# Hybrid encoder block: v's second half between the keys, the substitution beside z, query decays made in the scans

## Chip, cores and metric

The kernel runs on one core of one Trainium2 chip. The metric is the device time of one execution in microseconds; the value given is the median of three timed runs. A profile of one more execution goes with it.

## What is computed

One layer of an encoder block over 1024 tokens of width 1024, all in float32: a half step of SwiGLU, a mixer, another half step of SwiGLU, and a final row norm. The change is in the mixer and in the row norms.

```python
x = x + 0.5 * swiglu(rmsnorm(x, ffn1_norm), ...)
h = rmsnorm(x, mix_norm); p = h @ w_in
u_a, v_a, qkv, z, b_raw, a_raw = split(p)
# group A: layernorm of gelu(v), 8 groups x 64, a 128x128 causal matrix per group over 128 tokens
y_a = gelu(u_a) * (W_s @ layernorm(gelu(v_a), ln_g, ln_b) + b_s)
# group B: 4 heads x 128, chunks of 64 tokens
q, k, v = silu(causal_dwconv(qkv, conv_w)); q, k = l2norm(q), l2norm(k)
decay = exp(g_i - g_j) for i >= j
L = strict_lower(beta * (k @ k.T) * decay)        # solved: (I + L) sol = rhs, per chunk
u_c, w_c = sol(beta * v), sol(beta * k * exp(g))
attn = lower((q @ k.T) * decay)
# scan over chunks: v_new = u - w S;  o = (q exp(g)) S + attn v_new;  S = S exp(g_last) + k_dec.T v_new
x = x + concat(y_a, rmsnorm(o) * silu(z)) @ w_out
x = x + 0.5 * swiglu(rmsnorm(x, ffn2_norm), ...);  return rmsnorm(x, final_norm)
```

## The kernel before

Every large matmul is made from three float32r products (high times high, high times low, low times high), so weights and activations are split into a high and a low part: a cast on ScalarE (ACT) and a subtraction on VectorE (DVE). `split` does that (L61, L62). TensorE (PE) does the products (L53), GpSimd (POOL) small elementwise work, SyncE (SP) issues most transfers. The two feed-forward blocks (`ffn`) run before and after the mixer; the mixer is `middle`, from about 690 to 1077 us of the span. A tile framework draws all semaphores and orders each engine's instructions at compile time, by the order in which the program states them and by its own estimate of when each is ready. Each engine works through its queue in that order.

In `middle`, `hT` holds the transposed activations. `token_steps` makes 256 columns of a projection for eight tiles of 128 tokens, 24 matmuls of 128x256 each; `proj_steps` makes one 128-wide block of q, k or v for all 1024 tokens, in two halves of 24 matmuls of 128x512, each followed by a causal convolution: a copy into `pad` on ACT (L869), four passes on DVE (L871, L873), a Silu on ACT (L875). Weights come through `load_w` (a transfer, then a split, four buffers `wk`).

The order of the work is this:

1. v's first 256 columns (`v0`), spilled to DRAM; meanwhile beta and the log decays, and `decay(h)` for the four heads. Per head and half it makes two 512-wide tables from a row `grb` that a transfer spreads over the partitions: `EL` for the keys and `EA` for the queries, each by a subtraction, an addition and one Exp (L797 to L803). The two halves share the additions between DVE and POOL.
2. `keys(h)` for four heads: the key projection, two tiles of z's second half as filler (`fill`), then for both halves the transposes (L844), a squared norm on ACT (L896), 1/norm (L880 on DVE, the power L70 on POOL), scalings (L898 to L903), the Gram product, the matrix L (L908), and stores to DRAM. The tiles of the keys are called `kst`.
3. The rest of z; `substitute`, 31 pairs of dependent DVE instructions (L920, L922) on 32x32 blocks that come back from DRAM in another layout, and go out again through DRAM (`xz_d`).
4. v's second 256 columns (`tm("v", 1, ...)`), each tile with Gelu and the layer norm `mix` (L1077 to L1084); per pair of tiles `spatial`, 16 matmuls and a bias (L1094).
5. The value and query projections of head 0, then the scans: eight halves, each with `inverse` (which needs the substitution's result, `Z`), `values`, `queries` and `scan`, woven by hand with the projections of the next heads and with u.

The banks of PSUM in the mixer: two for `ax` (transposes, `spatial`, small products), three for `mm` (projections), one each for `sc`, `sq` and `sd`. The pool `xp` has eight buffers of 128x1024, of which `EL` and `EA` took all; `kst` has three, `aT`, `rv` and `u` two each.

The row norm is `rstd_of`: Square with accumulation on ACT (L74), scale and epsilon on DVE (L76), power on POOL (L70). `fin` is the final norm; its last tile is done in two halves (L655 to L661).

Of the kernel before, what the change touches and what calls it, by code (L numbers as in the profile page):

```python
# [17 lines left out]
P = 128  # L18
# [12 lines left out]
def block_kernel(ctx: ExitStack, tc, a, out):  # L31
# [39 lines left out]

    def rstd_of(src, junk, n):
        ms = sm.tile([P, 1], F32, tag="ms", name="ms", bufs=4)
        nc.scalar.activation(junk, src, AF.Square, accum_out=ms)  # L74
        rs = sm.tile([P, 1], F32, tag="rs", name="rs", bufs=4)
        nc.vector.tensor_scalar(rs, ms, 1.0 / n, EPS, op0=ALU.mult, op1=ALU.add)  # L76
        rpow(rs, rs, 1)
        return rs
# [479 lines left out]
    with ExitStack() as f2:  # L558
# [85 lines left out]
        def fin(t, xt):  # L644
            o = gp.tile([P, D], F32, tag="gsp", name="o", bufs=7)
            if t < 7:
                normed(xt, st["gf"], o)
                nc.sync.dma_start(odram[t], o)
                return

            halves = slice(0, 512), slice(512, D)
            ms = sm.tile([P, 2], F32, tag="ms2", name="ms2")
            rs = sm.tile([P, 1], F32, tag="rs", name="rs", bufs=4)
            for i, f in enumerate(halves):
                nc.scalar.activation(o[:, f], xt[:, f], AF.Square, accum_out=ms[:, i:i + 1])  # L655
            nc.gpsimd.tensor_tensor(rs, ms[:, 0:1], ms[:, 1:2], op=ALU.add)
            nc.gpsimd.tensor_scalar(rs, rs, 1.0 / D, EPS, op0=ALU.mult, op1=ALU.add)
            rpow(rs, rs, 1)
# [19 lines left out]
def middle(tc, nc, a, L):  # L678
# [4 lines left out]
    bank, mm, mm3, split, rpow = L["bank"], L["mm"], L["mm3"], L["split"], L["rpow"]  # L683

    csa = kp.tile([P, NCONST - 1, P], F32, tag="kst", name="csa", bufs=3)
    nc.scalar.dma_start(csa, a["cst"][:, P:].rearrange("p (c n) -> p c n", n=P))
# [97 lines left out]
    EL, EA = {}, {}  # L784

    def decay(h):
        EL[h], EA[h] = (xp.tile([P, 2, 512], F32, tag="x", name="E") for _ in range(2))
        for hf in range(2):
            cs = slice(h * 8 + hf * 4, h * 8 + hf * 4 + 4)
            grb = lv.tile([P, 512], F32, tag="VT", name="grb", bufs=4)  # L790
            nc.sync.dma_start(grb, grd[:, cs.start * P:cs.stop * P].to_broadcast([P, 512]))
            lv_, av_ = v4(EL[h][:, hf]), v4(EA[h][:, hf])

            def mask(i):
                return K(i).unsqueeze(1).to_broadcast([P, 4, P])

            nc.vector.tensor_tensor(av_, v4(grb), b4(gc[:, cs]), op=ALU.subtract)  # L797
            eng = nc.vector if hf else nc.gpsimd
            eng.tensor_tensor(lv_, mask(C_ML), v4(grb), op=ALU.subtract)
            eng.tensor_tensor(lv_, lv_, b4(gc[:, cs]), op=ALU.add)  # L800
            nc.scalar.activation(lv_, lv_, AF.Exp)
            nc.vector.tensor_tensor(av_, av_, mask(C_MA), op=ALU.add)
            nc.scalar.activation(av_, av_, AF.Exp)  # L803
# [81 lines left out]
    def keys(h, fill):  # L885
        kst = [kp.tile([P, 3, 512], F32, tag="kst", name="kst", bufs=3) for _ in range(2)]
        proj_conv(4 + h, [k[:, 0] for k in kst])
        for _ in range(2):
            next(fill, None)
        for hf in range(2):  # L890
            KT, kd, rw = (kst[hf][:, i] for i in range(3))
            cs = slice(h * 8 + hf * 4, h * 8 + hf * 4 + 4)
            kps = fourT(lambda t: KT[:, tl(t)])
            ssk = small("ssk")
            for t in range(4):
                nc.scalar.activation(rw[:, tl(t)], kps[:, tl(t)], AF.Square, accum_out=ssk[:, t:t + 1])  # L896
            rk = inv_norm(ssk, 1.0, EPS, "k")
            nc.gpsimd.tensor_tensor(brk[:, cs], beta[:, cs], rk, op=ALU.mult)  # L898
            br2, bw = small("br2"), small("bw")
            nc.gpsimd.tensor_tensor(br2, brk[:, cs], rk, op=ALU.mult)  # L900
            nc.gpsimd.tensor_tensor(bw, br2, ex[:, 0, cs], op=ALU.mult)
            nc.vector.tensor_tensor(v4(kd), v4(kps), b4(ex[:, 1, cs]), op=ALU.mult)
            nc.vector.tensor_tensor(v4(rw), v4(kps), b4(bw), op=ALU.mult)  # L903
            nc.sync.dma_start(kst_d[h * 2 + hf].rearrange("p (a n) -> p a n", a=3), kst[hf])
            gps = four(lambda t: KT[:, tl(t)], lambda t: KT[:, tl(t)], (ps_s, ("sc", "sd")[hf]))
            Lm = big("aT", 2)
            for t in range(4):
                nc.vector.scalar_tensor_tensor(Lm[:, tl(t)], gps[:, tl(t)], br2[:, t:t + 1], EL[h][:, hf, tl(t)], op0=ALU.mult, op1=ALU.mult)  # L908
            nc.sync.dma_start(full(Ld, h * 2 + hf), v4(Lm))

    def substitute():
# [5 lines left out]
        for j in range(31):  # L917
# [4 lines left out]
            nc.vector.tensor_tensor(X[:, j + 1:, :w], X[:, j + 1:, :w], tv, op=ALU.subtract)  # L922
# [3 lines left out]
        nc.sync.dma_start(xz_d[1], Z.rearrange("p r c -> p (r c)"))  # L926


    class Half:
# [57 lines left out]
        def values(self):  # L987
# [6 lines left out]
            nc.scalar.copy(self.u, up)  # L994
            yield

        def queries(self):
            q = self.wq[:, :, P:256]
            aT = self.aT = big("aT", 2)
            nc.scalar.activation(v4(aT), q, AF.Square)  # L1000
            ssq = bank(ps_a, "ax")[:, :4]
            for t in range(4):
                for c in (0, 64):
                    mm(ssq[c:c + 64, t:t + 1], aT[:, t * P + c:t * P + c + 64], ones, start=True, stop=True)
# [3 lines left out]
            nc.vector.tensor_tensor(aT, aps, EA[self.h][:, self.hf], op=ALU.mult)  # L1008
# [50 lines left out]

    def gm_consts():  # L1060
# [246 lines left out]
```

## Time and profile before

| | |
|---|---|
| median of three timed runs | 1849.43 us (1847.9 to 1852.1) |
| profiled execution, its own time | 1841.22 us |
| span of its trace | 1839.4 us |
| PE busy | 1784.1 us (97%) |
| DVE busy | 1191.7 us (65%) |
| POOL busy | 747.9 us (41%) |
| ACT busy | 686.6 us (37%) |
| mean granted PE clock | 0.992 |

Times in the rows count from the span's start. A row of the view of stretches has: the stretch, its length, then for PE, PE's weight loads, DVE, ACT and POOL the busy time and the number of instructions, then the granted PE clock as a share of full speed, the share of the transfer engines that was busy, and GB/s. A row of the time line has: start, duration, engine, line, operation, the tiles (output <- inputs) with shape, and the number of instructions merged; in brackets the idle time before, and what ended it. A row of the groups has: line, engine, operation, tiles, shape, number | busy time, mean ns of one | idle time before, and what ended it. A row of the waits has: who waited for whom, us in total, times, longest. "x" beside a matmul counts passes: a float32 product of 128x128 shows as two.

### The profile page before, as it was taken

The page shows a single profiled execution, that of the slowest core. Times are in us where ns is not written, and L with a number is a line of the kernel's source. Part 1 is how long each engine was busy: PE and PEld are TensorE (multiplying, and loading weights), DVE is VectorE, ACT ScalarE, POOL GpSimd, SP SyncE. Part 2 cuts the span into 40 slices and gives each one's busy share as a digit, 9 for nine tenths or more (in the row PEclk, how much of TensorE's full clock was granted, in tenths as well). Part 3 has the DMA queues.
Part 4 walks back from the last instruction along what each step waited for, and adds up shares of the span by engine and source line. Part 5 has one row for each costly group of instructions (what it writes and reads, how often), then busy time and mean ns, then how long its engine had stood idle before and what let it go on. Part 6 is the DMA issues. An engine that isn't in the chain of part 4 may idle for free.

```text
span 1839.4 us, 25484 instructions
## 1 busy us (share of the span) xinstructions
PE 1784.1 (97%) x9735; PEld 1524.8 (83%) x9735; DVE 1191.7 (65%) x1531; ACT 686.6 (37%) x1193; POOL 747.9 (41%) x583
## 2 busy tenths in 40 slices
PE   5999999999999999898999999999999999999997
PEld 4888888888788889797788989988888888878886
DVE  6867676665565575769655344587776766656546
ACT  6333332333343454432344533452333323243433
POOL 4667666565140012212132420366666665614001
PEclk9999999999999999999999999999999999999999
DMA  5353443544957445453432254334535445495744
GB/s 196 108 175 136 162 152 134 184 158 163 339 188 258 155 177 164 140 195 100 133 94 67 90 197 136 109 104 165 178 132 171 144 154 188 142 344 185 264 142 149
DMA packets 134441, 302.26 MB, mean 164 GB/s; under 512 B 27408, under 2 KB 42032, under 8 KB 134320
## 3 DMA queue, kind: packets, MB, share of 16 engines
q1 hardware_dynamic: 131824, 296.20, 46.9%
q10 hardware_dynamic: 2496, 4.44, 0.8%
q8 instruction: 76, 1.25, 0.3%
q14 instruction: 45, 0.37, 0.1%
HBM read 208.83 MB, written 91.77 MB: 163 GB/s over the span
## 4 chain that ended last, share of the span: by engine, by line
PE 78%; DVE 8%; DMA 5%; POOL 4%; issue 3%; ACT 2%; SPq 0%; POOLq 0%; DVEq 0%; ACTq 0%
PE mm L53 43%; PE ax L53 32%; POOL s L191 1%; POOL t L278 1%; DMA left<-hq 1%; DVE acc L873 1%; PE ax L95 1%; PE sd L53 1%; DMA graw<-in_f1gu_dram 1%; POOL s L278 1%; PE sc L53 1%; DVE T L119 0%; DVE unit L62 0%; DVE wk L62 0%; DVE E L797 0%
## 5 line engine op out<-in xcount | busy, mean ns | idle before, releaser
L53 PE MATMUL mm<-unit 128*128 128x512 f32 x1056 | 244.9, 392 | 4.2 <-ACT unit L61 2.2
L53 PEld LDWEIGHTS mm<-unit 128*128 128x128 f32 x1056 | 198.8, 189 | 47.4 <-ACT unit L61 3.3
L191 POOL TENSOR_TENSOR s<-graw 128x512 f32<-128x512 f32 x84 | 130.3, 1551 | 262.9 <-DMA graw<-in_f2gu_dram 116.0
L62 DVE TENSOR_TENSOR ga<-graw,ga 128x512 fp32r<-128x512 f32 x134 | 155.9, 1166 | 99.9 <-ACT ga L61 99.2
L61 ACT CAST gs<-s 128x512 fp32r<-128x512 f32 x168 | 104.5, 622 | 301.8 <-PE mm L53 151.0
L62 DVE TENSOR_TENSOR unit<-left,unit 128x1024 fp32r<-128x1024 f32 x84 | 101.9, 1215 | 133.0 <-ACT unit L61 132.3
L53 PE MATMUL ax<-T,gs 128*128 128x512 f32 x792 | 183.1, 389 | 0.0
L53 PE MATMUL ax<-unit 128*128 128x512 f32 x792 | 180.5, 389 | 0.0
L53 PEld LDWEIGHTS ax<-T,gs 128*128 128x128 f32 x792 | 148.7, 188 | 30.8
L53 PEld LDWEIGHTS ax<-unit 128*128 128x128 f32 x792 | 148.7, 188 | 30.8
L62 DVE TENSOR_TENSOR gs<-s,gs 128x512 fp32r<-128x512 f32 x168 | 172.7, 1030 | 2.3
L53 PE MATMUL mm<-B,ga 128*128 128x512 f32 (+1 forms) x864 | 166.8, 347 | 3.3 <-ACT B L118 1.9
L61 ACT CAST unit<-left 128x1024 fp32r<-128x1024 f32 x84 | 82.5, 982 | 230.2 <-PE ax L53 100.5
L53 PE MATMUL mm<-T,gs 128*128 128x512 f32 x720 | 166.5, 389 | 0.0
L53 PEld LDWEIGHTS mm<-B,ga 128*128 128x128 f32 x864 | 139.5, 194 | 23.4 <-ACT B L118 2.5
L53 PEld LDWEIGHTS mm<-T,gs 128*128 128x128 f32 x720 | 135.2, 188 | 28.0
L70 POOL TENSOR_TENSOR rs<-rs,half 128x1 f32<-128x1 f32 (+1 forms) x29 | 19.2, 662 | 334.5 <-DVE rs L76 334.4
L53 PE MATMUL mm<-actT,wk 128*128 128x512 f32 x576 | 150.4, 403 | 0.0
L53 PE MATMUL ax<-B,ga 128*128 128x512 f32 x528 | 127.2, 390 | 1.4 <-DVE ga L62 1.4
L53 PE MATMUL mm<-wk,actT 128*128 128x256 f32 x960 | 123.5, 285 | 2.7 <-DVE wk L62 2.7
L53 PEld LDWEIGHTS mm<-wk,actT 128*128 128x128 f32 x960 | 117.4, 190 | 3.4 <-DVE wk L62 3.0
L53 PEld LDWEIGHTS mm<-actT,wk 128*128 128x128 f32 x576 | 103.6, 188 | 18.8
(239 smaller groups left out, 3046.0 us busy)
## 6 DMA issues: line engine op xcount, KB each, us to landing
left<-hq SPq DMA_DIRECT2D x70, 512.0 KB, 5.0
graw<-in_f1gu_dram SPq DMA_DIRECT2D x44, 512.0 KB, 5.4
wq<-t SPq DMA_DIRECT2D x44, 512.0 KB, 2.8
hq<-s SPq DMA_DIRECT2D x44, 512.0 KB, 3.1
graw<-in_f2gu_dram SPq DMA_DIRECT2D x44, 512.0 KB, 4.7
right<-wq SPq DMA_DIRECT2D x40, 512.0 KB, 4.8
wd<-in_f1wd_dram SPq DMA_DIRECT2D x22, 512.0 KB, 6.6
hq<-sg SPq DMA_DIRECT2D x22, 512.0 KB, 3.7
```

Source lines behind the costliest of these rows:

```text
L53: nc.tensor.matmul(*args, **kw)
L61: nc.scalar.copy(h, src)
L62: nc.vector.tensor_tensor(l, src, h, op=ALU.subtract)
L70: nc.gpsimd.tensor_tensor(o, i, half[:, :w], op=ALU.pow)
L95: nc.tensor.transpose(ps[:, i * P:(i + 1) * P], blk(i), ident)
L191: nc.gpsimd.tensor_tensor(f, u, v, op=op)
L278: nc.gpsimd.tensor_tensor(o, u, v, op=op)
L873: nc.vector.scalar_tensor_tensor(acc, pad[:, j:j + 512], cw[:, blk, j:j + 1], acc, op0=ALU.mult, op1=ALU.add)
```

## The change

- **Row norms.** The factor 1/n goes into the Square's scale, and epsilon and power run on POOL (`rsqrt`); DVE has no part in it. The same function serves the key norms and `mix`.
- **Decays.** `decay` makes only `EL`, by one subtraction; the log decay is added as the Exp's bias, so the Exp is cut into four of 128x128. The query table is made in `values` of each half, into `aT`, from its own transfer of the row; `queries` squares into an `rv` buffer.
- **Keys.** The loop over the halves becomes `key_half`; its Gram product comes directly behind the transposes, and the rest of its body is as before.
- **Order.** v's second half, with its Gelu and norm, is the filler between the halves of each head's keys; PE's order in that region is the order of the program (`manual_schedule`). Then come the four `spatial`, the weights of the first value projection, `substitute`, and z's second half with its copy on ACT. The DVE work of the first value projection is queued behind the last instruction of the substitution (`issue_after`).
- **Norm of v.** Gain and shift move behind the spatial product: `mix` ends with one Identity on ACT, `gm_shift` folds the shift and the bias into one table `C`, and `spatial` multiplies by the gain on DVE and adds `C` on POOL. v's tiles come from `xp`.
- **Final norm.** The last tile's second half goes first; tile 6 returns its last step as a function.

```diff
+    def rsqrt(o, i, add, w=1):
+        nc.gpsimd.tensor_scalar(o, i, add, None, op0=ALU.add)
+        rpow(o, o, w)
 def rstd_of(src, junk, n):
-        nc.scalar.activation(junk, src, AF.Square, accum_out=ms)
-        nc.vector.tensor_scalar(rs, ms, 1.0 / n, EPS, op0=ALU.mult, op1=ALU.add)
-        rpow(rs, rs, 1)
+        nc.scalar.activation(junk, src, AF.Square, scale=n ** -0.5, accum_out=ms)
+        rsqrt(rs, ms, EPS)
 def fin(t, xt):
-                normed(xt, st["gf"], o)
-                nc.sync.dma_start(odram[t], o)
-                return
-            halves = slice(0, 512), slice(512, D)
+                rs = rstd_of(xt, o, D)
+                def scaled():
+                    nc.vector.scalar_tensor_tensor(o, xt, rs, st["gf"], op0=ALU.mult, op1=ALU.mult)
+                    nc.sync.dma_start(odram[t], o)
+                if t == 6:
+                    return scaled
+                return scaled()
+            halves = slice(512, D), slice(0, 512)
...
-    csa = kp.tile([P, NCONST - 1, P], F32, tag="kst", name="csa", bufs=3)
-    nc.scalar.dma_start(csa, a["cst"][:, P:].rearrange("p (c n) -> p c n", n=P))
+    csa = kp.tile([P, NCONST - 2, P], F32, tag="kst", name="csa", bufs=3)
+    nc.scalar.dma_start(csa, a["cst"][:, P:C_MA * P].rearrange("p (c n) -> p c n", n=P))
+    cma = ts.tile([P, P], F32, tag="cma", name="cma")
+    nc.scalar.dma_start(cma, a["cst"][:, C_MA * P:])
...
+    def exponents(e, bias, n):
+        for t in range(4):
+            nc.scalar.activation(e[:, tl(t)], e[:, tl(t)], AF.Exp, bias=bias[:, n * 4 + t:n * 4 + t + 1])
 def decay(h):
-            nc.vector.tensor_tensor(av_, v4(grb), b4(gc[:, cs]), op=ALU.subtract)
-            eng = nc.vector if hf else nc.gpsimd
-            eng.tensor_tensor(lv_, mask(C_ML), v4(grb), op=ALU.subtract)
-            eng.tensor_tensor(lv_, lv_, b4(gc[:, cs]), op=ALU.add)
-            nc.scalar.activation(lv_, lv_, AF.Exp)
-            nc.vector.tensor_tensor(av_, av_, mask(C_MA), op=ALU.add)
-            nc.scalar.activation(av_, av_, AF.Exp)
+            rows_of(grb, h * 2 + hf)
+            (nc.vector if hf else nc.gpsimd).tensor_tensor(v4(EL[h][:, hf]), masked(K(C_ML)), v4(grb), op=ALU.subtract)
+            exponents(EL[h][:, hf], gc, h * 2 + hf)
...
+    def key_half(h, hf, kst):
+        KT, kd, rw = (kst[:, i] for i in range(3))
+        cs = slice(h * 8 + hf * 4, h * 8 + hf * 4 + 4)
+        kps = fourT(lambda t: KT[:, tl(t)])
+        gps = four(lambda t: KT[:, tl(t)], lambda t: KT[:, tl(t)], (ps_s, ("sc", "sd")[hf]))
+        ssk = small("ssk")
+        for t in range(4):
+            nc.scalar.activation(rw[:, tl(t)], kps[:, tl(t)], AF.Square, accum_out=ssk[:, t:t + 1])
+        rk = small("rk")
+        rsqrt(rk, ssk, EPS, 4)
...
+        nc.sync.dma_start(full(Ld, h * 2 + hf), v4(Lm))
+    def keys(h, w, fill):
+        together(proj_steps(4 + h, w, [k[:, 0] for k in kst]))
+        key_half(h, 0, kst[0])
+        together(islice(fill, 2))
+        key_half(h, 1, kst[1])
...
 def values(self):
+            aT = self.aT = big("aT", 2)
+            rows_of(aT, self.n)
+            nc.vector.tensor_tensor(v4(aT), masked(cma), v4(aT), op=ALU.add)
+            exponents(aT, ngc, self.n)
 def queries(self):
-            aT = self.aT = big("aT", 2)
-            nc.scalar.activation(v4(aT), q, AF.Square)
+            aT, sq = self.aT, big("rv", 2)
+            nc.scalar.activation(v4(sq), q, AF.Square)
-            nc.vector.tensor_tensor(aT, aps, EA[self.h][:, self.hf], op=ALU.mult)
+            nc.vector.tensor_tensor(aT, aps, aT, op=ALU.mult)
...
+    def gm_shift(gm):
+        for g in range(8):
+            mm(rows_[:, g:g + 1], wsT[g // 4][:, g % 4], ones, start=True, stop=True)
+        nc.scalar.copy(rw, rows_)
+        for g in range(8):
+            nc.scalar.activation(c, c, AF.Identity, bias=bs[:, g:g + 1], scale=rw[:, g:g + 1])
 def mix(t, v, gm):
-        nc.vector.tensor_scalar(rs, mv[:, 1:2], EPS, None, op0=ALU.add)
-        rpow(rs, rs, 1)
-        nc.vector.scalar_tensor_tensor(v, v, mv[:, 0:1], lng, op0=ALU.subtract, op1=ALU.mult)
-        nc.vector.scalar_tensor_tensor(v, v, rs, lnb, op0=ALU.mult, op1=ALU.add)
+        rsqrt(rs, mv[:, 1:2], EPS)
+        nc.gpsimd.tensor_scalar(nm, mv[:, 0:1], rs, -1.0, op0=ALU.mult, op1=ALU.mult)
+        nc.scalar.activation(v, v, AF.Identity, bias=nm, scale=rs)
 def spatial(t, Vs, gm):
-            nc.vector.tensor_tensor(
...
+            nc.vector.tensor_tensor(o, mp.rearrange("p (g t c) -> p g t c", g=4, t=2), each(lng), op=ALU.mult)
+            nc.gpsimd.tensor_tensor(o, o, each(C), op=ALU.add)
 def ev_v(gm, later):
-                Vt[t // 2] = kp.tile([P, 2, 512], F32, tag="kst", name="vm", bufs=3)
+                Vt[t // 2] = xp.tile([P, 2, 512], F32, tag="x", name="vm")
-                for g in later:
-                    g()
-                later[:] = [partial(spatial, t, Vs, gm)]
+                later.append(partial(spatial, t, Vs, gm))
...
-    fill = token_steps([a["wz1"][0], a["wz1"][1]], 256, spill("z", 1), hT)
-    for h in range(HEADS):
-        keys(h, fill)
-    together(fill)
-    substitute()
     gm = gm_consts()
+    gm_shift(gm)
     later = []
-    tm("v", 1, ev_v(gm, later))
+    fill = steps("v", 1, ev_v(gm, later))
+    with tc.manual_schedule(engines={PE}):
+        for h in range(HEADS):
+            keys(h, load_qkv(4 + h), fill)
+        z1 = token_steps([a["wz1"][0], a["wz1"][1]], 256, spill("z", 1, nc.scalar.copy), hT, ahead=True)
+        next(z1)
+        for g in later:
+            g()
+        w8 = load_qkv(8)
+        last = substitute()
+        together(z1)
...
-    proj_conv(8, values_of(0))
-    later.pop()()
+    with tc.issue_after(last.ins):
+        together(proj_steps(8, w8, values_of(0)))
     proj_conv(0, queries_of(0))
```

## Rows read from the trace of the kernel before

**Rows 1.** Busy time of each engine in four stretches of the mixer.
```profile
743.00:757.00 14.00, 9.00 (x62) 8.66 (x62) 11.52 (x18) 7.94 (x24) 1.17 (x3) 0.88 0.35 114
757.00:812.00 55.00, 55.00 (x339) 49.32 (x338) 35.20 (x74) 15.92 (x52) 10.04 (x30) 1.00 0.47 160
812.00:863.00 51.00, 45.43 (x328) 42.02 (x326) 40.65 (x102) 14.84 (x37) 12.51 (x17) 1.00 0.51 152
893.00:1054.00 161.00, 159.75 (x1445) 136.74 (x1446) 78.97 (x175) 72.41 (x178) 51.86 (x62) 1.00 0.30 88
```

**Rows 2.** Waits of PE from 690 to 1056 us.
```profile
PE mm L53 <- DVE wk L62: 2.7, 1, 2.7
PE ax L844 <- ACT kst L875: 2.2, 1, 2.2
```

**Rows 3.** Time line from the last store of L to the first inverse.
```profile
821.18 0.37 SPq L909 DMA_DIRECT2D Ld<-aT  x1
...
830.97 0.21 DVE L920 TENSOR_TENSOR aT<-Lb,X 128x31 f32<-128x31 f32 x1 [0.22 <-DMA Lb<-Ld]
...
882.83 0.33 SPq L923 DMA_DIRECT2D xz<-X  x1
...
893.16 0.41 PE L53 MATMUL ax<-Z,L 32*32 32x32 f32 x8 [1.17 <-DMA Z<-xz]
```

**Rows 4.** Groups on PE, 700 to 1060 us: the matmuls of `spatial`.
```profile
L53 PE MATMUL ax<-vm,u 128*128 128x128 f32 x64 | 8.1, 280 | 5.6 <-DVE vm L1084 4.4 <-issue 1.2
```

**Rows 5.** Time line of PE: tiles of z behind two heads.
```profile
745.78 5.92 PE L53 MATMUL mm<-wk,actT 128*128 128x256 f32 x35 [2.75 <-DVE wk L62]
...
767.60 5.82 PE L53 MATMUL mm<-wk,actT 128*128 128x256 f32 x48
```

**Rows 6.** Busy time of each engine, two microseconds behind that wait.
```profile
748.00:750.00 2.00, 2.00 (x11) 2.00 (x11) 1.46 (x2) 0.47 (x1) 0.10 (x1) 0.50 0.78 254
```

**Rows 7.** Groups on DVE, 700 to 1060 us: decays and substitution.
```profile
L920 DVE TENSOR_TENSOR aT<-Lb,X 128x31 f32<-128x31 f32 (+15 forms) x31 | 10.4, 335 | 0.5 <-DMA Lb<-Ld 0.2
L797 DVE TENSOR_TENSOR E<-grb,gc 128x512 f32<-128x512 f32 x8 | 8.0, 1030 | 5.0 <-DMA grb<-grd 5.0
```

**Rows 8.** Groups on ACT, 700 to 1060 us: a pointer operand, an Exp.
```profile
L1040 ACT ACTIVATE ax<-oh,rq 128x128 f32<-128x128 f32 x32 | 11.9, 372 | 2.4 <-DVE oh L1037 1.8
L803 ACT ACTIVATE E<-E 128x512 f32<-128x512 f32 x8 | 5.0, 628 | 6.6 <-DVE E L802 6.4
```

**Rows 9.** Time line of PE: row sums by `ones` in the scans.
```profile
911.54 0.63 PE L53 MATMUL ax<-ones,aT 128*64 128x1 f32 x16
```

**Rows 10.** Time line of the heads: a Silu of half 0, a key projection.
```profile
766.70 0.63 ACT L875 ACTIVATE kst<-acc 128x512 f32<-128x512 f32 x1 [3.70 <-DVE acc L873]
...
775.83 11.17 PE L53 MATMUL mm<-actT,wk 128*128 128x512 f32 x48
```

**Rows 11.** A stretch of the last scans, and table loads in it.
```profile
1014.00:1046.00 32.00, 32.00 (x302) 31.00 (x302) 11.42 (x29) 17.42 (x35) 12.54 (x15) 1.00 0.30 92
...
1015.49 1.28 ACT L1118 ACT_TABLE_LOAD   x1
1016.79 0.38 ACT L1118 ACTIVATE ev<-mm 128x256 f32<-128x256 f32 x1
```

**Rows 12.** Time line of the last head: transposes of both halves, and L903.
```profile
811.73 0.60 PE L844 MATMUL ax<-ident,kst 128*128 128x128 f32 x4
...
813.06 0.60 PE L844 MATMUL ax<-ident,kst 128*128 128x128 f32 x4
...
815.67 0.69 DVE L903 TENSOR_TENSOR kst<-ax,bw 128x512 f32<-128x512 f32 x1 [1.37 <-POOL bw L901]
```

**Rows 13.** Time line of the tail: steps of the final norm.
```profile
1829.98 0.61 ACT L655 ACTIVATE o<-x 128x512 f32<-128x512 f32 x1
1830.11 0.15 DVE L76 TENSOR_SCALAR rs<-ms 128x1 f32<-128x1 f32 x1 [1.22 <-ACT o L74]
...
1834.06 0.19 POOL L657 TENSOR_SCALAR rs<-rs 128x1 f32<-128x1 f32 x1
```

## What the change does to the time: the prediction

> **What bounds the kernel now.** I read the engines' shares first. TensorE (PE) is busy for 97% of the span, so only PE's idle time, PE's clock, or PE work taken out can shorten it. This change takes no matmul out. So I next cut the mixer into stretches [rows 1] and looked where PE stood still. 743 to 757 us has 9.00 of 14.00 us busy: 5.0 us idle. 757 to 812, three of the four heads of `keys`, has 55.00 of 55.00. 812 to 863, v's second half, has 45.43 of 51.00: 5.6 us idle. 893 to 1054, the scans, has 159.75 of 161.00.
>
> The table of waits names the ends [rows 2]: the split of z's weights on VectorE (DVE) 2.7 us and the Silu of a key on ScalarE (ACT) 2.2 us. Later 1.2 us go to the transfer that brings the substitution's result back [rows 3]. The 5.6 us stand before the matmuls of `spatial` [rows 4], behind the norm (L1083, L1084) that DVE finishes late, because `substitute` shares DVE with it. All these ends are one complaint: DVE is late, in the first case with the decays, in the second with the norm.
>
> A stall also costs clock. After the 2.75 us wait, 35 matmuls of z took 5.92 us, where 48 of the same shape later took 5.82 us [rows 5]; between them the granted clock stood at 0.50, its lower level of 1.2 GHz [rows 6]. 35 at the later pace are 4.24 us, so 1.7 us were lost.
>
> The most that the change can win is therefore 5.0 + 5.6 + 1.2 + 1.7 = 13.5 us.
>
> **The change, part by part.**
>
> *Decays.* `decay` loses the query half: DVE no longer issues L797 and L802, sixteen instructions near 1.0 us each [rows 7], nor L800, whose add becomes the bias of the Exp. That is what z's weights and the first head's convolution queued behind. I count the 5.0 us and the 1.7 us as gone (they come back if DVE is still late; nothing else that I see stands there). ACT pays: four Exp of 128x128 with a bias pointer for one Exp of 128x512. The nearest row with a pointer operand is 0.372 us; one of 128x512 took 0.628 [rows 8]. So 1.49 us for 0.63, eight times, +6.9 us on ACT before the heads. ACT's Exps had waited for DVE there, 6.6 us before L803 alone, so this is hidden by time in which ACT stood idle; without that cover the first head's `pad` copies would be late by as much. The constants come in two transfers instead of one, an extra issue on ACT's queue before PE needs any of it: nothing.
>
> *`gm_shift`.* Eight calls with one column, 16 matmuls. Sixteen such (row sums by `ones`) took 0.63 us [rows 9]. Between 0, if they fall into a stall, and 0.6; I take 0.6. Its copy and eight small Identities on ACT come while ACT is idle.
>
> *Heads.* PE's order is now fixed as written: 48 matmuls of a key, then at once the transposes and the Gram product of half 0, two tiles of v, then half 1. Half 0's Silu therefore loses its cover. Before, 5.8 us of z stood there. A Silu that began at 766.70 and took 0.63 ended 0.27 us before the key's matmuls did [rows 5, 10]; so it just fits. Now Gelu stands between the Silus and ACT must load a table for each turn: 1.28 us [rows 11]. If ACT meets it while DVE still convolves, it costs PE nothing. Queued behind PE's wait are the Gram product, both v tiles, and half 1. Bounds: 0 and (1.28 - 0.27) = 1.0 per half 0, with as much and 0.3 more for half 1 in the worst case. DVE is lighter (no copy of z, no L1083 and L1084), so I take 0.4 per head, 1.5 in all. The rsqrt goes from DVE and POOL to POOL alone, which costs nothing that PE sees. v's Identity (two pointers) runs on ACT in place of two DVE passes, the loads of v and the stores of `sp["m"]` move ahead on SP's queue, z's stores behind; an issue there is 0.37 us [rows 3] and SP has room.
>
> *Spatial.* Its four blocks stand right after the last head. Their 64 matmuls take 8.1 us [rows 4], about 1.0 per bank, with two banks. One bank is still held by the last transposes until L903 has read it. For the half before, that was 811.73 to 816.36: 4.6 us [rows 12]. PE spends 1.3 on transposes and Gram product (811.73 to 813.06 in the same rows) and 1.0 on the first bank, so it would wait 2.3 us. Lower bound 0 (what follows the region, the value projection, may be put in between), upper bound 4.6 (the last v tile's norm late as well). I take 2.3 of the 5.6 us.
>
> *Substitution.* Its own work is 31 pairs of L920 and L922, 10.4 us each line [rows 7], 20.8 us; before, it was stretched from 830.97 to 882.83 [rows 3]. From the last transposes: 4.6 us to L903, about 1.5 for L908, 9.8 from the store of L to the first pair (821.18 to 830.97), 20.8, then 10.3 to the first matmul that reads Z (882.83 to 893.16): 47 us. PE's cover: 1.3 + 8.1 + 2.3 + z 192 matmuls at 0.121 us = 23.3 [rows 5], and two projections of 48 at 11.2 us [rows 10] = 22.4; together 57. The slack of 10 us is about what DVE must still do in between (eight evacuations of `spatial`, five weight splits). I take 0; bounds 0 and 3, since the next projection can be pulled forward as it is now. `issue_after` only holds the value projection's convolution back, for which PE does not wait until the scans.
>
> *Query decays in the scans.* Each of eight halves gets a transfer, one masked add on DVE, four Exps on ACT (1.49 us), and up to two table loads, Exp and back to Silu, 2 x 1.28. So ACT gets up to 4.05 us per half, 32 us on its 72 of 161 [rows 1]. The squares for the query norm now use a `rv` buffer, which is free only after the values' product. Nothing of this is wanted by PE at once except through ACT's queue: behind the Exps stand the copies of `inverse` and of u, which PE does wait for. Lower bound 0: 1014 to 1046 had five table loads (one is shown) and PE was busy 32.00 of 32.00 us [rows 11]. Upper bound: PE waits out half of each block, 16 us. The nearest row is the former; I take 1.5.
>
> The Trainium skill, in ScalarE: Activation LUTs (What ACT_TABLE_LOAD costs), gives about 2.66 us for every switch of set, load and drain together, and its Rules for kernel authors say to do all calls of one set before the next. The change does the reverse; by that price ACT's addition would be 54 us and the upper bound 27. The trace doesn't agree on the drain: the load began at 1015.49 and the Gelu behind it at 1016.79, 1.30 us later [rows 11].
>
> *Norms elsewhere, and the tail.* DVE's 0.15 us step becomes a POOL step of 0.19 [rows 13], so a row norm is about 0.1 us longer, at the start and at the end where it is exposed: 0.3. The last tile's second half already has its Square ahead of the first half's (L655 at 1829.98), so the swapped halves give nothing. `t == 6` returns a function that the loop calls in the same step, so nothing is deferred.
>
> **The sum.** 13.5 - (0.6 + 1.5 + 2.3 + 0 + 1.5 + 0.3) = 7.3 us. The profiled execution took 1841.2 us (span 1839.4), 8.2 below the median of the timed runs, 1849.43; taking the same difference off the median: 1842.1 us.
>
> **The rivals.**
>
> *PE's fixed order gives the gain back (no change).* In the heads PE can no longer step around a late key. Speaking for it: the 0.27 us margin, and Gelu and Silu by turns. Against: 55.00 of 55.00 us busy before with DVE more loaded. At both bounds, 1.0 + 1.3 per head, 9.2 instead of 1.5: 1849.8. It eats the gain above the measurable from 1.3 us per head.
>
> *The table loads in the scans (slower).* ACT's in-order queue puts 4.05 us ahead of a copy that PE needs, in each half. With half of it exposed, 16 instead of 1.5 us: 1856.6. Even is reached at 1.1 us per half, measurably slower at 1.6. For it: the scans have no stall to give back. Against: the five loads without idle time [rows 11], and that the projections which PE now does before 893, while it waits for Z, are left to fill the scans. The Trainium skill's ScalarE: Activation LUTs (Rules for kernel authors), which wants calls batched by set, stands on this rival's side.
>
> *All covers hold (faster still).* Only the 0.6 is paid: 1836.5.
>
> *The substitution isn't in one piece.* The edge binds one convolution; evacuations, splits and the next convolutions may still get between. Then Z is late by up to 3 us: 1845.1, still faster.
>
> **How the numbers follow.** A measurement tells about 0.2%, 3.7 us, from no change: faster is below 1845.7, slower above 1853.1. The forecast and the cases near it (all covers hold, Z late) have 0.62; the fixed order, and smaller losses that add up to it, 0.24; the scans 0.10 and any other loss of that size 0.04. The range goes from the case in which all covers hold, less 1.5 for the spread of the timed runs, 1835, to 1851.5, past the fixed order's case; what lies beyond is most of the slower cases. The forecast alone: 1838 to 1846.
>
> **What would show it.** After: no wait of PE on `wk` or `kst` in the first head, clock 1.00 there; 77 us for the four heads; a PE wait near 2 us at the second bank of `spatial`, ended by L903; L920 and L922 within some 25 to 33 us; PE without idle time up to the first matmul on Z; ACT at some 65% in the scans with PE still above 98%. Wrong would be waits before the key transposes in every head, or PE idle behind ACT copies next to table loads in the scans.

## The result, and the profile after

The changed kernel takes 1857.13 us (median of six runs, 1853.5 to 1858.3) where the kernel before takes 1847.91 beside it. The ratio is 1.0037, interval [1.0024, 1.0051]: slower by some 6.8 us. The medians lie 9.2 us apart; here and below, what is won or lost is worked out from the ratios, 0.1% being 1.85 us. The forecast was 1842.1, with 1851.5 as its upper end.

The mixer of the changed kernel in five stretches (the columns are those of [rows 1]; the first head, three heads, `spatial` and z, the first inverse, the scans):

```profile
core 0: us, PE busy (x) PEld busy (x) DVE busy (x) ACT busy (x) POOL busy (x), PEclk, DMA share, GB/s
735.00:756.00 21.00, 19.38 (x119) 17.00 (x119) 12.54 (x20) 20.65 (x45) 3.02 (x8) 1.00 0.47 154
756.00:815.00 59.00, 58.71 (x366) 52.02 (x365) 38.31 (x76) 39.19 (x89) 20.84 (x54) 1.00 0.40 138
815.00:866.00 51.00, 44.63 (x317) 41.62 (x317) 34.59 (x78) 14.51 (x32) 16.61 (x20) 0.97 0.63 193
866.00:895.00 29.00, 25.15 (x161) 19.53 (x160) 19.10 (x34) 14.62 (x24) 0.88 (x5) 0.82 0.41 123
895.00:1056.00 161.00, 159.51 (x1363) 135.68 (x1359) 88.20 (x179) 109.60 (x220) 48.20 (x58) 1.00 0.29 85
```

The first head now loses 1.6 us instead of 5.0, at full clock. The scans are as full as before: 159.51 of 161 us, with ACT at 68%. The loss stands between them: 6.4 us in the stretch of `spatial` (5.6 before), and a new one of 3.85 us at the first inverse, where the granted clock also falls. PE's waits in the mixer, against [rows 2] and [rows 4]:

```profile
PE ax L53 <- DVE kst L912: 3.9, 1, 3.9
PE ax L53 <- ACT rv L975: 3.8, 1, 3.8
PE ax L53 <- DVE vm L1129: 2.5, 3, 1.4
PE ax L856 <- ACT kst L887: 1.8, 2, 1.6
PE sc L53 <- DVE S L1052: 1.1, 2, 0.6
PE ax L53 <- ACT rv L1020: 0.3, 1, 0.3
```

The first is a bank of PSUM that the last head's transposes, at 813.84 us, hold until L912 has read it. Ahead of that stand, on ACT and then DVE:

```profile
813.56 1.28 ACT L1141 ACT_TABLE_LOAD   x1
814.85 0.38 ACT L1141 ACTIVATE vm<-mm 128x256 f32<-128x256 f32 x1
816.38 0.81 ACT L1115 ACTIVATE vm<-vm,bmv,brs 128x512 f32<-128x512 f32 x1 [1.14 <-POOL bmv L1114]
817.10 0.26 ACT L904 ACTIVATE kst<-ax 128x128 f32<-128x128 f32 x1
```

```profile
821.23 0.69 DVE L912 TENSOR_TENSOR kst<-ax,bw 128x512 f32<-128x512 f32 x1 [1.58 <-POOL bw L910]
```

The second one is a copy inside `inverse`. This is ACT's time line up to it (start, length, then the instruction; a bracket gives idle time before it):

```profile
873.47 1.28 ACT L807 ACT_TABLE_LOAD   x1 [1.58 <-DMA aT<-grd]
...
875.19 1.28 ACT L887 ACT_TABLE_LOAD   x1
876.48 0.63 ACT L887 ACTIVATE VT<-acc 128x512 f32<-128x512 f32 x1
877.02 0.57 ACT L881 COPY pad<-mm 128x512 f32<-128x512 f32 x1
877.60 1.28 ACT L807 ACT_TABLE_LOAD   x1
...
880.27 1.04 ACT L61 CAST wk<-raw 128x1024 fp32r<-128x1024 f32 x1
881.32 1.28 ACT L887 ACT_TABLE_LOAD   x1
882.62 0.63 ACT L887 ACTIVATE wq<-acc 128x512 f32<-128x512 f32 x1
883.15 0.52 ACT L975 COPY rv<-ax 32x128 f32<-32x128 f32 x2
```

PE had the first matmuls on Z done by 876 and then had 15 matmuls of a projection, until 879.6; the copy began at 883.15. ACT worked all that time, on Silus, Exps and their tables, two `pad` copies and a cast, which its queue holds ahead of the copy. Behind the stall PE runs at half clock for 8 us:

```profile
878.00:882.00 4.00, 1.60 (x8) 0.98 (x6) 3.86 (x7) 3.97 (x7) 0.31 (x1) 1.00 0.73 229
882.00:886.00 4.00, 2.56 (x22) 1.75 (x23) 2.84 (x5) 2.27 (x5) 0.00 (x0) 0.62 0.67 245
886.00:890.00 4.00, 4.00 (x27) 3.04 (x26) 0.28 (x1) 0.95 (x2) 0.15 (x1) 0.50 0.11 23
890.00:894.00 4.00, 4.00 (x30) 3.43 (x29) 3.07 (x5) 0.60 (x2) 0.14 (x2) 0.60 0.05 8
```

The second surprise lies outside the mixer. The norm's new POOL step (L74) takes 0.22 us alone. At the kernel's start, and again with the last weights of the second feed-forward block, it takes 1.1 to 1.3, each time next to a norm product on DVE (L86, L654) or a split. At the start, alone, and beside a product that runs from 11.08 to 12.36:

```profile
10.16 0.22 POOL L74 TENSOR_SCALAR rs<-ms 128x1 f32<-128x1 f32 x1 [3.16 <-ACT f L79]
...
11.20 1.24 POOL L74 TENSOR_SCALAR rs<-ms 128x1 f32<-128x1 f32 x1 [0.16 <-ACT f L79]
```

DVE, then POOL, with those last weights:

```profile
1820.73 1.29 DVE L654 SCALAR_TENSOR_TENSOR o<-x,rs,grow 128x1024 f32<-128x1024 f32 x1 [0.77 <-POOL rs L70]
1822.78 1.28 DVE L654 SCALAR_TENSOR_TENSOR o<-x,rs,grow 128x1024 f32<-128x1024 f32 x1 [0.77 <-POOL rs L70]
1824.83 1.28 DVE L654 SCALAR_TENSOR_TENSOR o<-x,rs,grow 128x1024 f32<-128x1024 f32 x1 [0.77 <-POOL rs L70]
1826.03 1.22 DVE L62 TENSOR_TENSOR unit<-left,unit 128x1024 fp32r<-128x1024 f32 x1
```

```profile
1820.78 1.32 POOL L74 TENSOR_SCALAR rs<-ms 128x1 f32<-128x1 f32 x1
1822.17 0.57 POOL L70 TENSOR_TENSOR rs<-rs,half 128x1 f32<-128x1 f32 x1
1822.83 1.31 POOL L74 TENSOR_SCALAR rs<-ms 128x1 f32<-128x1 f32 x1
```

The step for the next tile starts with DVE's product for the last one and ends only when that has ended; the power follows, and DVE stands for 0.77 us. The products thus begin 2.05 us apart, of which DVE works 1.28. Before, DVE stood for the power too, but for less: 0.44 and 0.66 us ahead of two of the four products, and not at all ahead of the others. So the weight split (L62) queued behind the four is late, PE waits 1.95 us for it (0.53 at the same place before), and the granted clock stands at 0.57 from 1828 to 1832. The Trainium skill, in SBUF — State Buffer (Who interferes with whom), says that a DVE instruction with two SBUF inputs and a GpSimd instruction that reads SBUF exclude each other for their whole length. The 1.31 us agree with it, and an estimate by that rule would have priced this norm step at the 1.28 us of DVE's product ([rows 13] have 0.15 for the step on DVE).

### The profile page after: what moved, and what is told of

It is laid out like the page before. It is cut to its first block, busy times and chain, and to the rows that moved or that the text cites. A ratio compares the mean times of both kernels' runs of the same rounds, so it can differ in the third digit from the quotient of the medians.

```text
span 1856.5 us, 25627 instructions
## 1 busy us (share of the span) xinstructions
PE 1794.8 (97%) x9751; PEld 1531.1 (82%) x9751; DVE 1156.2 (62%) x1453; ACT 762.6 (41%) x1310; POOL 761.1 (41%) x638
## 5 line engine op out<-in xcount | busy, mean ns | idle before, releaser
L61 ACT CAST gs<-s 128x512 fp32r<-128x512 f32 x168 | 104.3, 622 | 301.6 <-PE mm L53 136.8
L62 DVE TENSOR_TENSOR ga<-graw,ga 128x512 fp32r<-128x512 f32 x134 | 148.6, 1112 | 109.4 <-ACT ga L61 108.9
L62 DVE TENSOR_TENSOR unit<-left,unit 128x1024 fp32r<-128x1024 f32 x84 | 101.3, 1209 | 143.4 <-ACT unit L61 143.4
L62 DVE TENSOR_TENSOR gs<-s,gs 128x512 fp32r<-128x512 f32 x168 | 179.1, 1068 | 4.0 <-ACT gs L61 1.7
L61 ACT CAST unit<-left 128x1024 fp32r<-128x1024 f32 x84 | 82.4, 982 | 239.7 <-PE ax L53 102.6
L74 POOL TENSOR_SCALAR rs<-ms 128x1 f32<-128x1 f32 x27 | 15.4, 571 | 326.5 <-ACT xn L79 136.3
L53 PEld LDWEIGHTS ax<-B,ga 128*128 128x128 f32 x528 | 100.0, 190 | 23.4 <-DVE ga L62 2.6
```

Of the source, the lines that this page charges most:

```text
L53: nc.tensor.matmul(*args, **kw)
L61: nc.scalar.copy(h, src)
L62: nc.vector.tensor_tensor(l, src, h, op=ALU.subtract)
L74: nc.gpsimd.tensor_scalar(o, i, add, None, op0=ALU.add)
```

## The experiments

Each ratio is to the kernel before, from runs beside it on the same chip. The first three columns of the table are each profiled execution cut at z's first matmul and at the first transpose behind u's projection (us).

| kernel | to z | mixer | rest | ratio [95%] |
|---|---|---|---|---|
| before; again (e0) | 681.9; 684.6 | 395.2; 397.9 | 762.2; 765.1 | 0.9996 [0.9968, 1.0024] |
| changed | 685.1 | 400.5 | 770.9 | 1.0037 [1.0024, 1.0051] |
| e8, before with the decays | 681.8 | 390.1 | 767.0 | 0.9951 [0.9937, 0.9965] |
| e2, before with norm on POOL | 684.5 | 403.5 | 769.3 | 1.0039 [1.0016, 1.0063] |
| e1, changed with norm on DVE | 682.4 | 398.3 | 768.7 | 1.0007 [0.9987, 1.0026] |
| e10, changed with order free | 686.2 | 391.6 | 769.1 | 0.9984 [0.9964, 1.0005] |
| e17, e10 with norm on DVE | 681.7 | 391.2 | 767.6 | 0.9957 [0.9936, 0.9978] |

**The kernel before again.** One execution says little here: 29 runs of the kernel before reached from 1842.5 to 1862.2 us.

> The kernel before itself, unchanged, timed against itself and profiled a second time. Ratio 1.000; the half-width of the interval is what a comparison here can tell. The profiled execution of before took 1841.2 us, well under its median, so the second profile should be some 5 to 8 us longer; if the longer part is the feed-forward part behind the mixer (762.2 us from the end of u's projection to the last instruction, 770.9 in the changed kernel), those 8.7 us are no loss of the change.

Half of that held: the second profile has a span 8.2 us longer, but only 2.9 of it behind the mixer. So of the 8.7 us which the changed profile loses there, part only is the change's.

**The norm's step, back on DVE, and alone in the kernel before.**

```diff
-        nc.scalar.activation(junk, src, AF.Square, scale=n ** -0.5, accum_out=ms)
+        nc.scalar.activation(junk, src, AF.Square, accum_out=ms)
...
-        rsqrt(rs, ms, EPS)
+        nc.vector.tensor_scalar(rs, ms, 1.0 / n, EPS, op0=ALU.mult, op1=ALU.add)
+        rpow(rs, rs, 1)
```

> The changed kernel, but the row norm's step before the power is back on VectorE (one tensor_scalar with both numbers) as in the kernel before; the power stays on POOL. Theory A (the loss has two places, the norm step of 128x1 that POOL finishes late beside VectorE's wide instructions, and the first inverse, where a copy stands on ScalarE behind Exps and table loads): the stretch before z gets back the 3.2 us that it lost, so about 1851.7 where the changed kernel has 1854.8 (1.0037 of before); perhaps 1 us more from the norms behind the mixer. Theory B (all of the loss is table loads in the scans, and the 3.2 us ahead of z are a difference between two executions): no change, 1854.8. Theory C (the hand-made order of TensorE is the loss): no change.

> The kernel before with one part of the change alone: the row norm's epsilon step on POOL instead of VectorE. Theory A: 3 us slower than before, near 1851 (1.0016), all of it ahead of z and in the second feed-forward part. Theories B and C: no change, 1848, ratio 1.000.

1852.74 (1.0007) and 1855.91 (1.0039). Both say that the step costs: 0.30% or 5.5 us by the first, 7 by the second, each with some 4.4 us either way. It shows at the start (the first matmul on `ga` at 16.31 us in e1, 17.29 in the changed kernel), and at the last weights of the second feed-forward block. PE's last 82 matmuls in the changed kernel, then in e1:

```profile
1827.30 20.52 PE L53 MATMUL mm<-unit 128*128 128x512 f32 x82 [1.95 <-DVE unit L62]
```

```profile
1821.13 18.92 PE L53 MATMUL mm<-unit 128*128 128x512 f32 x82 [0.37 <-DVE unit L62]
```

1.58 us of wait and 1.60 of clock: 3.2 of the 5.5 us stand here alone. Both marks stand in every profile of this record: in the nine kernels with the step on POOL the matmul on `ga` begins at 17.2 to 17.3 us and that wait is 1.7 to 2.0; in the nine with it on DVE, 16.2 to 16.4 us and 0.3 to 0.5.

**The decays' part alone.** `decay` and the query half in `values` as in the change, all else as before.

> The kernel before with the decays' part of the change alone: the key decays with one subtraction and four Exps with a bias, the query decays made in each half of the scans; heads, spatial, substitution and norms as before. Theory A with the first inverse (Exps in the scans cost only where ACT is piled up): the first head's 5.0 us of idle time and 1.7 us of clock are won, 45 table loads for 16 cost 2 us: about 1845, ratio 0.997 to 0.998. Rival (table loads in every half): 1.1 us and more for each of eight halves eats the gain, ratio 1.001 or more.

1837.55: 9.1 us faster than before. PE's waits in its mixer:

```profile
PE ax L53 <- DVE vm L1091: 6.0, 2, 3.1
PE ax L53 <- issue: 1.1, 1, 1.1
PE sc L53 <- DVE S L1039: 0.9, 2, 0.6
```

`wk` and `kst` of [rows 2] are gone, and 45 table loads in place of 16 cost nothing that shows: in its scans, 887 to 1048 us, PE is busy 160.08 of 161. So the change is not slow by the decays alone.

**The first inverse: what stands ahead of its copy.** In e3 Exp becomes Identity with scale 0, so the kernel leaves out the exponential of the query decays; in e7 the Exps are queued behind the inverse:

```diff
-            nc.scalar.copy(self.wq[:, :, 0:P], v4(wps))
+            self.inv = nc.scalar.copy(self.wq[:, :, 0:P], v4(wps))
...
-            exponents(aT, ngc, self.n)
+            with tc.issue_after(self.inv.ins):
+                exponents(aT, ngc, self.n)
```

> The changed kernel with the query decays' Exp replaced by Identity (with scale 0 and the same bias pointer): the exponential of the query decays is left out, everything else stays, so ScalarE needs no Exp table after the heads (31 table loads instead of 60). Theory A: the 3.85 us stall at the first inverse and the 4 us of half clock behind it go, other halves hardly change: about 1847, minus 7.5, and the stretch from z's start to the first inverse stays. Theory B (every half pays about 1 us for its table loads): also minus 7, but the seven later halves get shorter and the first inverse doesn't. Theory C: 2 us at most.

> The changed kernel, its arithmetic whole; each half's four query Exps are only queued on ScalarE behind the last copy of the same half's inverse, so none stands ahead of the first inverse's first copy. About as many table loads (56 for 60). Theory A (place, not number): the first inverse's stall and its half clock go, 5 to 7.5 us faster than the changed kernel, 1847 to 1850. Theory B (number): no change, 1854.8. A middle case: the Exps now come late for the score product of that half and PE waits there, some 1 us each, 1854.

e3: 1855.29, 1.0028 [1.0012, 1.0043]; the wait for the copy is still 3.0 us. e7: 1851.49, 1.0003 [0.9988, 1.0018], and 1.8 us. So my first explanation, Exps and their tables, falls: without any Exp the copy is still late, behind two Silus, a `pad` copy and a cast:

```profile
877.18 0.63 ACT L887 ACTIVATE VT<-acc 128x512 f32<-128x512 f32 x1
...
880.27 0.63 ACT L887 ACTIVATE wq<-acc 128x512 f32<-128x512 f32 x1 [1.88 <-DVE acc L885]
880.81 0.57 ACT L881 COPY pad<-mm 128x512 f32<-128x512 f32 x1
881.27 1.05 ACT L61 CAST wk<-raw 128x1024 fp32r<-128x1024 f32 x1
882.22 0.53 ACT L975 COPY rv<-ax 32x128 f32<-32x128 f32 x2
```

The later Silu had itself waited 1.88 us for DVE's convolution, which comes behind the substitution.

> The changed kernel with both mends at once: the row norm's step back on VectorE and the query Exps queued behind the inverse. Alone they stood at 1.0007 and 1.0003 of before, where the changed kernel stands at 1.0037. If they are independent the sum is 0.9973, 1845; if both are one and the same slack, 1.000.

1849.49, 1.0012 [1.0002, 1.0023], with 2.7 us at the copy: by the ratio not the sum, and nothing beyond e1 or e7. Its profile says otherwise: both marks of the norm's step are gone (16.22 us, and 0.37 of wait), and its mixer takes 396.4 us, as e7's 396.5. Between e7 and e11 the step has no price by the ratios, where three other pairs give it 0.27 to 0.39% (e1, e2, and e17 against e10). Why this pair differs stays open, and so does what e7's gain was.

**The value convolution let go** (`issue_after(last.ins)` taken out).

> The changed kernel without the rule that holds the first value convolution behind the substitution on VectorE. Theory E: the four convolution halves no longer pile up between the substitution's end and the first inverse, so ScalarE's Silus are done before the inverse's copy is wanted; the 3.85 us stall and the half clock behind it go, though Z comes up to 3 us later: ratio 1.001. Theory D: no change, 1.0037.

1862.42, 1.0057 [1.0036, 1.0078]: not faster, and slower by its profile (a mixer of 407.9 us), though the interval overlaps that of the changed kernel. The wait is 2.4 us, and 0.6 for Z comes to it; the granted clock was 0.69 from 875 to 895 and 0.63 from 895 to 915. My expectation was wrong, and nothing speaks for taking the rule out.

**z ahead of `spatial`** (two of its eight blocks), and in e15 with it the stores of `spatial` on POOL's queue, where they don't stand in front of the substitution's load.

```diff
-        next(z1)
+        together(islice(z1, 3))
...
-        nc.sync.dma_start(sp["m"][t - 1:t + 1].rearrange("t p n -> p t n"), Vs)
+        nc.gpsimd.dma_start(sp["m"][t - 1:t + 1].rearrange("t p n -> p t n"), Vs)   # e15 only
```

> The changed kernel with two of z's eight blocks (48 matmuls, 5.8 us) put between the last head and the spatial matmuls in the order written for TensorE; nothing else changes. Theory A: the 6.4 us that PE waits in the spatial stretch (3.9 of them for the bank that the last transposes hold) go to 1 or less, up to 5 us faster, 1850. Rival: the substitution's result is no earlier, so PE stands at the first inverse instead and the gain is given back there: 1854 to 1856, with the wait at the first inverse's copy grown by as much.

> The changed kernel with two of z's blocks ahead of spatial (alone 1.0014 of before, with 4.0 us of TensorE waiting for the substitution's result) and with spatial's stores issued from POOL's queue, so that the load of the substitution's matrix doesn't stand behind four stores on SyncE's queue. That load is issued some 8 us earlier; the 4.0 us wait for the substitution's result goes: 4 us less than with the blocks alone, ratio 0.999. Rival: the substitution then meets spatial's evacuations on VectorE and ends hardly earlier: 1.0014 again.

1850.21, 1.0014 [1.0003, 1.0025], and 1853.69, 1.0011 [0.9993, 1.0030]. The waits of e14, then of e15:

```profile
PE ax L53 <- DMA Z<-xz: 4.0, 1, 4.0
PE ax L53 <- DVE vm L1129: 2.7, 1, 2.7
```

```profile
PE ax L53 <- ACT rv L975: 3.9, 1, 3.9
PE ax L53 <- DVE vm L1129: 2.7, 1, 2.7
```

The bank's 3.9 us are gone in both, and a wait of the same length takes their place: for Z itself, and once Z is earlier, for the inverse's copy. By the ratios some 4 us are won, hardly clear of the noise; the rest is passed on.

**The order of PE left to the scheduler,** throughout, and from the end of the heads on.

```diff
-    with tc.manual_schedule(engines={PE}):
-        for h in range(HEADS):
-            keys(h, load_qkv(4 + h), fill)
+    for h in range(HEADS):
+        keys(h, load_qkv(4 + h), fill)
...
```

> The changed kernel without the hand-made order: TensorE's queue is ordered by the scheduler from the due times, as in the kernel before; all else stays. Theory D (the rearranged first half costs some 10 us against the decays' part alone, and most of it is the fixed order: 6.4 us of waits before spatial's matmuls, 1.8 before key transposes, the first inverse's stall): 5 us or more faster than the changed kernel, ratio 1.001 or less. Theory E (the cost lies in what is queued on VectorE and ScalarE behind the undivided substitution, whatever TensorE's order): the spatial wait goes but the time comes back at the first inverse, 1.003 to 1.004.

> The changed kernel with the hand-made order closed behind the last head: the heads stay as written, spatial, z and what follows are left to the scheduler. If the order's 0.53% lies behind the heads (spatial's waits of 6.4 us, the first inverse's 3.85 us stall and its half clock): 0.9984 as with the order left free throughout. If it lies in the heads (each key's transposes right behind its matmuls): 1.003.

1848.64, 0.9984, and 1846.54, 0.9984 [0.9962, 1.0006]: the fixed order costs 0.53%, 9.8 us with some 4.5 either way, and none of it shows in the heads. e10 in the two stretches of `spatial` and the first inverse:

```profile
816.00:866.00 50.00, 44.46 (x307) 41.41 (x307) 33.67 (x74) 14.05 (x31) 15.65 (x18) 0.97 0.63 190
866.00:896.00 30.00, 29.98 (x224) 23.23 (x222) 21.46 (x42) 13.80 (x26) 0.68 (x5) 1.00 0.44 124
```

`spatial` is no better: z goes between its blocks (2.0 us for the bank, 0.7 for `vm`), but one wait of 2.8 us for z's copy on ACT comes in, which itself waits for the store of an earlier tile. The gain is at the inverse: 29.98 of 30 us at full clock, where the changed kernel had 25.15 of 29 at 0.82. ACT's queue there:

```profile
876.87 1.28 ACT L807 ACT_TABLE_LOAD   x1
878.16 0.40 ACT L807 ACTIVATE aT<-aT,na 128x128 f32<-128x128 f32 x1
878.57 0.54 ACT L975 COPY rv<-ax 32x128 f32<-32x128 f32 x2
...
880.03 1.04 ACT L61 CAST wk<-raw 128x1024 fp32r<-128x1024 f32 x1
...
882.38 1.15 ACT L887 ACTIVATE wq<-acc 128x512 f32<-128x512 f32 x2
```

The copy now has its place in front of the Silus of the queries and the cast. The edit touches PE's order alone, and an entry on another engine's queue has moved; that the framework lays out each queue from its estimate of the rest is the likely reason. No run moves the copy with PE's order kept, so that its place makes the gain is read from these two time lines.

**All together, and two variations.** e17: order free, row norm on DVE. e19: also the Exps behind the inverse. e20: order free, every epsilon step on DVE.

> The changed kernel with TensorE's order left free (alone 0.9984 of before) and the row norm's step back on VectorE (alone 1.0007). If the three parts add up (decays -0.49%, norm step on POOL near +0.30%, fixed order near +0.53%) it stands at 0.9954, equal to the kernel before with the decays' part alone (0.9951). If norm step and order share one slack: 0.998.

> The changed kernel with order free, the row norm's step on VectorE, and the query Exps queued behind their half's inverse. With the order free there is no stall at the first inverse left to win, so it equals the one without the last edit, 0.9954; if Exps ahead of the inverse's copies still cost in later halves, 0.993.

> The changed kernel with order free and the epsilon step of every reciprocal root (row norms, keys, v, the tail) on VectorE. If the row norms alone carry the norm's loss, it equals order free with the row norm on VectorE, 0.9954; if the keys' and v's small POOL steps cost in the heads too, 0.994; if VectorE, in order, now holds these steps up in the heads, 0.997.

1842.09 (0.9957), 1842.45 (0.9964 [0.9942, 0.9986]) and 1842.40 (0.9957 [0.9933, 0.9982]). The parts add up (0.9954 was the sum); the small steps of keys and v on POOL cost nothing that shows, and neither does the Exps' place.

**The decays with v's new norm, at its old place** behind the substitution.

> The kernel before with the decays' part (alone 0.9951) and v's norm, shift and spatial evacuation as changed (three POOL steps, one Identity on ScalarE, the shift by 16 one-column matmuls), but at their old place behind the substitution, with TensorE's order left free. Theory D: v's norm on ScalarE no longer shares VectorE with the substitution, the 6.0 us of waits before spatial's matmuls go to 1 or 2, less 1.8 for the 16 matmuls: ratio 0.993. Theory E, with POOL's small steps stretched beside VectorE's two-input instructions to 1 us and more each: the norm is as late as before, 0.996.

1859.76, 1.0044 [1.0026, 1.0062], 17 us behind e8. PE waits 6.8 us for v's Identity on ACT and 3.1 for Z, and the clock stands at 0.50 from 892 to 916. The new norm does no harm between the keys (e17); here it does. The time line shows a part of it: before L1119, the product with the gain, DVE stands 2.61 us for PE (from 826.01 to 828.62) and again 2.53, with the substitution's pairs and the statistics of the next tiles of v queued behind it. Whether that is the whole cause no run separates.

## Why the prediction was wrong

The measured parts: decays -9.1 us, the norm's step +5.5 (e1), the fixed order +9.8 (e10), and e17 against e8, +0.06% or 1.1 us, for all the rest of the rearrangement. That is +7.3; measured are +6.8. Of this sum one thing is a test, that norm and order add up: 15.3 us by their own runs, 14.9 from e17 to the changed kernel. Each part is uncertain by 2.6 (decays) to 4.7 us.

- **Decays**: right, and too small. I had 5.0 + 1.7 less 1.5 for the scans, 5.2; alone they brought 9.1. By the profiles the mixer became 5.1 us shorter than in the first one of the kernel before and 7.8 than in the second, so part of the 9.1 may be noise. Both waits in the first head and its half clock went. In the scans nothing shows: the rival of table loads, whose 1856.6 happens to lie on the result, is refuted by e8. The Trainium skill's rule to batch by set (ScalarE: Activation LUTs, Rules for kernel authors) asks for the opposite of what e8 does; there its breach cost nothing that shows.
- **Norms elsewhere**, 0.3: the step that failed worst for its size. I compared the lengths of two instructions, 0.15 and 0.19 us, and didn't ask what DVE does while POOL works. The step measured 5.5 (e1), the tail's later tiles included, since POOL's step lasted as long as the product on DVE beside it; only behind PE's last matmul did the move help (8.7 us to the end instead of 9.3).
- **Substitution**, 0: in what it watched this was right. The pairs took 26.1 us, 841.18 to 867.28, and PE had no idle time between `spatial` and the first matmul on Z. But the stall came one step later, at the copy between two small products, which I had named only for the scans: 3.85 us and then half clock.
- **`spatial`**, 2.3: mis-sized. 6.4 us, more than the 5.6 before. I took the 4.6 us that L903's product needed before; now Gelu, a table load and v's Identity stand ahead of the Squares, from 813.56 on, so the bank of the transposes of 813.84 is free only when L912 ends, 8.1 us later.
- **Heads** 1.5 and **`gm_shift`** 0.6: the waits of the heads came to the forecast size, 1.8 us before the keys' transposes. But 1.62 of it lie in the first head, where ACT is busy 20.65 of 21 us: with Exps, with Gelus and their tables, and with the eight Identities of `gm_shift`, 2.76 us, for which I had taken ACT to be idle. The matmuls of `gm_shift` took 1.84 us, 0.11 each rather than 0.04. The four heads took 79.9 us against a forecast of 77.
- **The rival of PE's fixed order** (1849.8, the gain given back) named the right edit with the wrong mechanism. I priced late keys in the heads, which cost nothing that shows (e18); the traces show the cost behind them, above all at the copy of the first inverse. That its 9.2 comes near the measured 9.8 is luck.

With either of the two mended the kernel can't be told from the one before (1.0007, 0.9984). So the forecast failed at two terms: the norm, put at nearly nothing, and the order, put at 1.5 in the heads and at nothing for the copies behind them. I had no case with both.

Two versions beat both kernels: the decays' part alone (0.9951), and the whole change with the order free and the row norm's step on DVE (0.9957; e19 and e20 stand beside it). These two can't be told apart, so v between the keys and the undivided substitution bring nothing that shows here. Open are the profiles' differences behind the mixer: up to 4.8 us in the second feed-forward block between kernels that are equal there (645.1 before, 649.9 in e8), with a wait for a weight cast (L61) and half clock behind it. In 17 of the 18 profiles that wait takes 1.9 to 2.8 us, in the second one of the kernel before too; the one without it (0.2) is the first, from which I had predicted.

## What to carry to other kernels

A small step moved from a busy engine to an idle one must be priced beside what the first engine then runs: here POOL's 0.22 us became 1.31 beside a product on DVE with two inputs in SBUF, and the chain of product, step and power went at 2.05 us, about the sum of the three. An order fixed by hand on one engine can also rearrange the queues of the others, as it did here, so look at what stands ahead of the next short copy that PE needs, not only at PE. And price a stall with its clock: behind the 3.85 us the small products of the first inverse, 48 passes from the copy on, kept PE busy for 5.6 us, and for 3.4 in e10, which has no stall there.

## What the hardware showed that I had not expected

A POOL step on 128x1 took 0.22 us alone and 1.31 beside a 128x1024 product on DVE. After a stall of 3.85 us PE's granted clock stood at half, 1.2 GHz, for 8 us; after one of 3.1 us, in e16, for 24 us (892 to 916), with PE busy nearly all the time. ACT's 45 table loads of 1.28 us each, some 58 us, found room in idle time and did not show in the time of e8.
